# Hybrid encoder step on one core: x loaded first, three cached-key buffers, and another form of the delta rule's norms and sum

## The chip, the cores and the metric

The kernel is one program on one core of one Trainium2 chip. The time is that of one execution on the device, in microseconds; three runs of the kernel before gave 2281.72, 2284.39 and 2290.14 us. The engines are TensorE (PE, with PEld for its weight loads), VectorE (DVE), ScalarE (ACT), GpSimd (POOL) and SyncE (SP, which here only issues DMAs).

## What is computed

One inference step of a one-layer hybrid encoder on 2048 prompt tokens and 8 x 16 sample tokens: an input projection, a gated delta rule (group A, 4 heads), sparse attention whose keys an indexer picks (group B), attention into a memory (group C), and an output projection. The change is in group A and around the sample's indexer. The delta rule, per head and chunk:

```python
kb = k * beta[..., None]
lmat = jnp.where(strict, einsum('bnhid,bnhjd->bnhij', kb, k) * decay, 0.0)
rhs = concatenate([v * beta[..., None], kb * exp(gc)[..., None]], axis=-1)
sol = triangular_solve(lmat + eye(chunk), rhs, left_side=True, lower=True)
u0, wk = sol[..., :dv], sol[..., dv:]
def step(s, xs):
    u = u0_c - einsum('bhcd,bhde->bhce', w_c, s)
    o = einsum('bhcd,bhde->bhce', qd_c, s) + einsum('bhij,bhje->bhie', qk_c, u)
    s = s * last_c[..., None, None] + einsum('bhcd,bhce->bhde', kd_c, u)
```

q and k are first scaled to unit length over their 128 channels. The indexer scores every token t against every key s with `sum_h w[t,h] relu(q_idx[t,h].k_idx[s])`; for the 8 samples s runs over 4096 cached keys each.

## The kernel before

All is float32; a product that must be exact to float32 is made of a high and a low part of each operand (xh, xl, wh, wl, three products). The 17 token tiles of 128 rows (tile 0 holds the samples) go in five groups of 4, 4, 3, 3 and 3 tiles. For each group, 15 steps of projections run (`steps`); each projects into PSUM tile pp and hands on to post-processing. A head's four projections are k, q and then v, z (`t_step`), with channels on the partitions.

The delta rule of a head goes through three stages. **a** (`delta_a`, L991): the squares of k and q are made by ACT from SBUF (sq), a product with a column of ones sums them over the partitions into one column of PSUM tile pa for each tile and operand (pn), DVE takes the reciprocal root; then the decays, Lp (k.k with decay) and at (k.q with decay), and the inverse of each 16 x 16 diagonal block, through DMAs to DRAM and back. **b** (`delta_b`, L1095), for one or two tiles at a time: k is transposed (pk in PSUM tile pb); kw is it times nbe (minus beta, the norm and the decay), kd is it times the decay to the chunk's end; cv is v transposed and scaled; three levels grow the inverse's transpose Z to 128 x 128; nw is the product of kw and Z. **c** (`delta_c`, L1159): for each prompt tile, u = Z.cv + nw.S in PSUM tile pl, then the output and the new state S (Sst). Stage a of head n+2, and its first projections, are recorded only behind stage c of head n.

The samples' index (`idx_sample`, L723) takes 64 blocks of cached keys. `cache_keys` (L701) loads a block (raw, two buffers), ACT copies its high part into kc (two buffers), DVE subtracts the low part, PE multiplies, ACT makes the relu.

The order of the work is fixed when the program is built. Streams (generators) of the stages run against a clock made of a table of costs (`weave`, L173, and `Paced`): the stream that is earliest by it records its next instructions, a yield of some nanoseconds sets it back, and an entry's "lag" (LAG, 600 ns, unless it has its own) is the time that is left between a step and its user. Every engine then takes its instructions in the order of the record, SP its DMAs too. `norms` (L314) sums the squares of x by ACT, half a tile at a time, for the mean over channels; `prep` (L328) scales the transposed x by the result and splits it into xh and xl. L169 is the line of the helper through which all compute instructions are recorded, so rows are told apart by tile names.

After the groups (at some 1550 us) the attention and the output projection follow in pools of their own.

## Time and profile before

| | |
|---|---|
| median of 3 runs | 2284.39 us |
| profiled execution | 2285.57 us |
| its span, first to last instruction | 2283.8 us |
| PE busy | 2006.2 us (88%) |
| DVE busy | 1651.3 us (72%) |
| ACT busy | 1290.8 us (57%) |
| POOL busy | 421.6 us (18%) |
| mean granted TensorE clock | 0.938 of 2.4 GHz |

A busy share is a mean over stretches that differ; the rows below are therefore by stretch, by tile or by time. "Idle before" is the time that the engine stood in front of an instruction, with the one that ended it behind the arrow. Matmuls overlap in the array, so that the mean length of one is more than the time it takes from its engine; a run of several tells the latter.

### The profile page before, as it was taken

How to read it: one execution, taken by the hardware profiler on the slowest of the kernel's cores; microseconds unless marked ns; L12 is line 12 of the kernel's file. 1: busy time of each engine (PE TensorE's matmuls, PEld its weight loads, DVE VectorE, ACT ScalarE, POOL GpSimd, SP SyncE). 2: the span in 40 equal slices, each digit the busy share in tenths (PEclk: the TensorE clock that was granted, in tenths of full speed). 3: DMA queues.
4: the chain of work that ended last, by engine and by line, in shares of the span. 5: the costliest groups of instructions: out<-in, count | busy, mean ns of one | idle time of the engine just before them, and what ended most of it. 6: DMA issues, size and time to landing. Idle time of an engine off the chain costs nothing.

```text
span 2283.8 us, 43471 instructions
## 1 busy us (share of the span) xinstructions
PE 2006.2 (88%) x14123; PEld 1637.8 (72%) x14123; DVE 1651.3 (72%) x6571; ACT 1290.8 (57%) x3193; POOL 421.6 (18%) x494
## 2 busy tenths in 40 slices
PE   3876968688899998999899899989999999999984
PEld 2755746677688888888788888966776666777752
DVE  3766655556888788889988899687767787655541
ACT  3454555445545666566756765456756667545430
POOL 3341512211121101211111111132211121111000
PEclk9886979788999998999899999999999999999996
DMA  7687667866544455556555555547876776765642
GB/s 230 185 246 212 225 156 215 206 224 200 190 162 164 159 183 200 199 192 222 186 212 196 202 193 215 189 138 242 244 227 209 230 222 208 246 207 187 198 137 81
DMA packets 323533, 453.25 MB, mean 198 GB/s; under 512 B 81760, under 2 KB 230880, under 8 KB 303840
## 3 DMA queue, kind: packets, MB, share of 16 engines
q1 hardware_dynamic: 322976, 449.32, 62.2%
q8 instruction: 114, 1.87, 0.3%
q0 software_dynamic: 320, 1.06, 0.2%
q14 instruction: 123, 1.01, 0.1%
HBM read 344.53 MB, written 105.75 MB: 197 GB/s over the span
## 4 chain that ended last, share of the span: by engine, by line


## 5 line engine op out<-in xcount | busy, mean ns | idle before, releaser
L169 PE MATMUL pp<-wh,xh 128*128 128x256 f32 (+1 forms) x952 | 289.3, 304 | 8.5 <-ACT v L169 3.8
L169 PE MATMUL pp<-wl,xh 128*128 128x256 f32 (+1 forms) x952 | 280.3, 295 | 1.2 <-POOL wl L169 1.2
L169 PE MATMUL pp<-wh,xl 128*128 128x256 f32 (+1 forms) x952 | 279.8, 295 | 1.3 <-DVE xl L169 1.3
L169 PE MATMUL pp<-xh,wh 128*128 128x384 f32 (+1 forms) x640 | 249.6, 390 | 10.1 <-ACT wh L169 3.6
L169 ACT ACTIVATE relu<-pi 128x512 f32<-128x512 f32 (+3 forms) x340 | 183.4, 545 | 112.6 <-PE pi L169 65.7
L169 PE MATMUL pp<-xh,wl 128*128 128x384 f32 (+1 forms) x640 | 242.8, 380 | 2.4 <-DMA wl<-wd2l 1.7
L169 DVE SCALAR_TENSOR_TENSOR score<-relu,w,score 128x512 f32<-128x512 f32 (+3 forms) x304 | 221.9, 731 | 30.7 <-ACT relu L169 16.6
L169 PE MATMUL pp<-xl,wh 128*128 128x384 f32 (+1 forms) x640 | 242.8, 379 | 0.0
L169 PEld LDWEIGHTS pp<-wh,xh 128*128 128x128 f32 x952 | 186.2, 196 | 12.9 <-ACT v L169 4.3
L169 PEld LDWEIGHTS pp<-wl,xh 128*128 128x128 f32 x952 | 186.3, 196 | 4.6 <-issue 1.7
L169 PEld LDWEIGHTS pp<-wh,xl 128*128 128x128 f32 x952 | 185.3, 195 | 5.0 <-DVE xl L169 2.5
L169 ACT ACTIVATE junk<-score,tf 128x1024 bf16<-128x1024 f32 (+11 forms) x126 | 142.6, 1132 | 69.0 <-DVE tf L169 45.5
L169 POOL TENSOR_TENSOR Lm<-Lp,cf 128x256 f32<-128x256 f32 (+1 forms) x120 | 85.4, 712 | 309.9 <-PE pb L169 284.1
L169 PE MATMUL pi<-kstack,qst 128*128 128x512 f32 (+3 forms) x304 | 128.4, 430 | 13.9 <-ACT relu L169 11.3
L169 PEld LDWEIGHTS pp<-xh,wh 128*128 128x128 f32 x640 | 125.9, 197 | 20.0 <-ACT wh L169 3.8
L169 PEld LDWEIGHTS pp<-xh,wl 128*128 128x128 f32 x640 | 125.4, 196 | 14.9 <-DMA wl<-wd2l 2.2
L169 PEld LDWEIGHTS pp<-xl,wh 128*128 128x128 f32 x640 | 125.8, 197 | 8.2
L169 PE MATMUL py<-woh,mixh 128*128 128x512 f32 x272 | 122.8, 451 | 3.7 <-ACT mixh L169 3.7
L169 POOL TENSOR_TENSOR wl<-wr,wh 128x512 fp32r<-128x512 f32 (+1 forms) x61 | 81.0, 1336 | 212.3 <-ACT wh L169 205.0
L169 PE MATMUL py<-woh,mixl 128*128 128x512 f32 x272 | 110.7, 407 | 1.8 <-POOL mixl L169 1.8
L169 PE MATMUL py<-wol,mixh 128*128 128x512 f32 x272 | 110.3, 405 | 0.0
L169 POOL TENSOR_TENSOR mixl<-mixr,mixh 128x512 fp32r<-128x512 f32 x33 | 42.3, 1281 | 328.1 <-ACT mixh L169 252.3
(421 smaller groups left out, 5440.1 us busy)
## 6 DMA issues: line engine op xcount, KB each, us to landing
skt<-in_kT SPq DMA_DIRECT2D x128, 256.0 KB
svt<-in_v SPq DMA_DIRECT2D x128, 256.0 KB
nraw<-in_x SPq DMA_DIRECT2D x34, 256.0 KB
xres<-in_x SPq DMA_DIRECT2D x34, 256.0 KB
part_d<-xres SPq DMA_DIRECT2D x34, 256.0 KB
xres<-part_d SPq DMA_DIRECT2D x34, 256.0 KB
out_y<-xres SPq DMA_DIRECT2D x34, 256.0 KB
mixr<-mixT_d SPq DMA_DIRECT2D x33, 256.0 KB
```

The lines of the kernel that those rows point to most:

```text
L169: return f(*args, **kw)
```

## The change

x is loaded first, into eight buffers (tiles of stage a that are free so early), and only the first 512 columns of the constant table follow; the rest and the small tables move into a stream of their own, `small_constants`, and the post-processing is recorded only behind it. The cached keys get a third raw and a third converted buffer, two of the converted ones in columns of kstack, and a lag of 2000 ns. In stage a, k and q are transposed by PE, and ACT's Square sums along each row of the transpose; kd is made there from the same transposes. For prompts kw and nw are gone: stage c forms r = nbe*(k.S) + cv by DVE and u = Z.r. The sample tile keeps kw and nw.

```diff
...
 NX = 2
 EARLY = 14
 NSEL = 256
-PRI1 = (0, 0, 0, 0, 0, 0, 0, 0, 0, 300, 0)
+PRI1 = (0, 0, 0, 0, 0, 0, 0, 0, 0, 0, 300, 0)
 PRI2 = (0, 0, 0, 0, 0, 0, 0, 0, 0)
 MASKED = -(2.0 ** 98)
 BIAS = -(2.0 ** 100)
...
     cpool = ctx.enter_context(tc.tile_pool(name="const", bufs=1))
     dpool = ctx.enter_context(tc.tile_pool(name="scratch", bufs=1, space=DRAM))
     cf = cpool.tile([128, CF_N], F32, name="cf")
-    nc.sync.dma_start(cf, a["cf"])
 
     def C(n):
         return cf[:, CF_COLS[n][0]:CF_COLS[n][1]]
     ident = C("ident")
-    nc.sync.dma_start(g_in, a["g_in"])
...
-    nc.sync.dma_start(cw, a["conv_w"])
-    V.tensor_scalar(cw, cw, 0.5, None, op0=OP.mult)
     g_o = cpool.tile([128, 1], F32, name="g_o")
-    nc.sync.dma_start(g_o, a["g_o"])
-    V.tensor_scalar(g_o, g_o, 0.5, None, op0=OP.mult)
     ab = cpool.tile([128, 8], F32, name="ab")
-    nc.sync.dma_start(ab, a["ab"].to_broadcast([128, 8]))
-    S.activation(ab[:, 0:4], ab[:, 0:4], AF.Exp)
-    V.tensor_scalar(ab[:, 0:4], ab[:, 0:4], -1.0, None, op0=OP.mult)
-    with tc.tile_pool(name="zero", bufs=1) as zp:
-        zero = zp.tile([128, 129], F32, name="zero")
-        G.memset(zero, 0.0)
-        for i in (1, 2):
-            for j in range(2):
-                nc.gpsimd.dma_start(blk_d[i][j].rearrange("t (p r) -> p t r", p=128), zero[:, None, :].to_broadcast([128, 4, 129]))
-
     b1 = ctx.enter_context(ExitStack())
     pi = ctx.enter_context(tc.tile_pool(name="pi", bufs=2, space=PSUM, side="right"))
     tp = ctx.enter_context(tc.tile_pool(name="tp", bufs=1, side="right"))
...
     Sst = gpool.tile([128, 4, 128], F32, name="Sst")
     V.memset(Sst, 0.0)
     gains = gpool.tile([128, 224], F32, name="gains")
-    nc.sync.dma_start(gains, a["gains"].to_broadcast([128, 224]))
-    for o in (0, 128):
-        V.tensor_scalar(gains[:, o:o + 64], gains[:, o:o + 64], 0.125, None, op0=OP.mult)
+
+    def small_constants():
+        yield 4000.0
+        nc.sync.dma_start(cf[:, 512:], a["cf"][:, 512:])
+        nc.sync.dma_start(ab, a["ab"].to_broadcast([128, 8]))
+        nc.sync.dma_start(gains, a["gains"].to_broadcast([128, 224]))
+        nc.sync.dma_start(cw, a["conv_w"])
+        nc.sync.dma_start(g_o, a["g_o"])
+        yield 9000.0
+        S.activation(ab[:, 0:4], ab[:, 0:4], AF.Exp)
+        V.tensor_scalar(ab[:, 0:4], ab[:, 0:4], -1.0, None, op0=OP.mult)
+        for o in (0, 128):
+            V.tensor_scalar(gains[:, o:o + 64], gains[:, o:o + 64], 0.125, None, op0=OP.mult)
+        V.tensor_scalar(cw, cw, 0.5, None, op0=OP.mult)
+        V.tensor_scalar(g_o, g_o, 0.5, None, op0=OP.mult)
+        done["cn"] = 1
     pp = b1.enter_context(tc.tile_pool(name="pp", bufs=2, space=PSUM, side="right"))
     pa = b1.enter_context(tc.tile_pool(name="pa", bufs=1, space=PSUM))
     pb = b1.enter_context(tc.tile_pool(name="pb", bufs=1, space=PSUM))
...
         ss = xp.tile([128, 5, 2], F32, name="ss")
         for t in range(n):
             for e in range(2):
-                xt = np_.tile([128, 512], F32, name="nraw")
+                if gi:
+                    xt = np_.tile([128, 512], F32, name="nraw")
+                else:
+                    xt = dp.tile([128, 4, 128], F32, name="xrow", tag=("Lp", "at", "X", "Z")[t]).rearrange("p a b -> p (a b)")
                 nc.sync.dma_start(xt, a["x"][(g0 + t) * 128:(g0 + t + 1) * 128, e * 512:e * 512 + 512])
                 S.activation(xt, xt, AF.Square, accum_out=ss[:, t, e:e + 1])
+        if gi == 0:
+            nc.sync.dma_start(cf[:, :512], a["cf"][:, :512])
+            nc.sync.dma_start(g_in, a["g_in"])
         sm = xp.tile([128, 5], F32, name="ssm")
         V.tensor_tensor(sm[:, :n], ss[:, :n, 0], ss[:, :n, 1], op=OP.add)
         V.tensor_scalar(sm[:, :n], sm[:, :n], 1.0 / D, EPS, op0=OP.mult, op1=OP.add)
...
         tp = keys["tp"]
 
         def fetch(i):
-            raw = keys["sc"][:, 1536:2048] if i % 2 else tp.tile([128, 512], F32, name="kraw", tag="junk")
+            raw = keys["sc"][:, 1536:2048] if i % 3 == 1 else tp.tile([128, 512], F32, name="kraw", tag=("junk", "", "far")[i % 3])
             nc.sync.dma_start(raw, a["kidxT"][order[i % 8], :, i // 8 * 512:i // 8 * 512 + 512])
             return raw
-        raws = [fetch(0), fetch(1)]
+        raws = [fetch(i) for i in range(3)]
         yield 3500.0
         for i in range(64):
-            yield from until(lambda: keys["n"] >= i - 1)
-            kc = tp.tile([128, 512], F32R, name="kc", tag=("qn", "far")[i % 2])
+            yield from until(lambda: keys["n"] >= i - 2)
+            kc = kstack[:, 512 + 512 * (i % 3):][:, :512] if i % 3 else tp.tile([128, 512], F32R, name="kc", tag="qn")
             S.activation(kc, raws[i], AF.Copy)
             yield 1
             V.tensor_tensor(kc[64:128], raws[i][64:128], kc[64:128].bitcast(F32), op=OP.subtract)
-            keys["k"].append({"x": kc})
+            keys["k"].append({"x": kc, "lag": 2000.0})
             yield keys["k"][-1]
-            if i + 2 < 64:
-                raws.append(fetch(i + 2))
+            if i + 3 < 64:
+                raws.append(fetch(i + 3))
 
     def idx_sample(tp, pl, top):
         yield from until(lambda: done["i"] > 0)
...
     def head_proj(n_, h, gi, w, parts_, R, hp):
+            yield from until(lambda: done["cn"])
...
         gs = slice(g0, g0 + n)
 
-        pn = pa.tile([128, 512], F32, name="pa")
+        ms = dp.tile([128, 12], F32, name="dms")
+        kd = dp.tile([128, 4, 128], F32, name="kd")
         for i, x in enumerate((k, q)):
-            for lo, hi in units(gi):
-                sq = t3(dp, "sq", hi - lo, bufs=2)
-                S.activation(sq, x[:, lo:hi], AF.Square)
-                yield 1
-                for t in range(lo, hi):
-                    T.matmul(pn[:, i * n + t:i * n + t + 1], sq[:, t - lo, :], C("one")[:, 0:1], start=True, stop=True)
-                yield 0
-        ms = dp.tile([128, 12], F32, name="dms")
-        V.tensor_scalar(ms[:, :2 * n], pn[:, :2 * n], EPS, None, op0=OP.add)
+            pn = p3(pa, n)
+            for t in range(n):
+                T.transpose(pn[:, t, :], x[:, t, :], ident)
+            yield 1
+            for t in range(n):
+                sq = dp.tile([128, 128], F32, name="sq", bufs=2)
+                S.activation(sq, pn[:, t, :], AF.Square, accum_out=ms[:, i * n + t:i * n + t + 1])
+                if i == 0:
+                    S.activation(kd[:, t], pn[:, t, :], AF.Copy, scale=esuf[:, g0 + t, h:h + 1])
+            yield 1
+        V.tensor_scalar(ms[:, :2 * n], ms[:, :2 * n], EPS, None, op0=OP.add)
         rr = dp.tile([128, 12], F32, name="drr")
         rsqrt(rr[:, :2 * n], ms[:, :2 * n], dp, "d%d" % n)
         rk, rq = rr[:, :n], rr[:, n:2 * n]
...
             Lms.append(Lm)
         for lv in levels[:2]:
             level(lv)
-        kw, kd, cv = t3(dp, "kw", m, bufs=1), t3(dp, "kd", m), t3(dp, "cv", m)
-        pk = p3(pb, m)
-        for t in range(m):
-            T.transpose(pk[:, t, :], k[:, lo + t, :], ident)
-        yield 1
-        V.tensor_tensor(kw, pk, nbe[:, lo:hi, None].to_broadcast(shp), op=OP.mult)
-        for t in range(m):
-            S.activation(kd[:, t], pk[:, t, :], AF.Copy, scale=esuf[:, g0 + lo + t, h:h + 1])
-        yield 1
+        cv = t3(dp, "cv", m)
+        if smp:
+            kw = dp.tile([128, 128], F32, name="kw", bufs=1)
+            pk = p3(pb, 1)
+            T.transpose(pk[:, 0, :], k[:, 0, :], ident)
+            yield 1
+            V.tensor_scalar(kw, pk[:, 0, :], nbe[:, 0:1], None, op0=OP.mult)
+            yield 1
         pv = p3(pb, m)
         for t in range(m):
             T.transpose(pv[:, t, :], v[:, lo + t, :], ident)
...
             if li == 0:
                 level(levels[2])
             yield 1
-        pw = p3(pb, m)
-        for t in range(m):
-            T.matmul(pw[:, t, :], kw[:, t, :], Zg[:, t, :], start=True, stop=True)
-        yield 1
-        nw = t3(dp, "nw", m)
-        S.activation(nw, pw, AF.Copy)
-        R[lo] = Zg, kd, cv, nw
+        nw = None
+        if smp:
+            pw = p3(pb, 1)
+            T.matmul(pw[:, 0, :], kw, Zg[:, 0, :], start=True, stop=True)
+            yield 1
+            nw = dp.tile([128, 1, 128], F32, name="nw", bufs=1)
+            S.activation(nw, pw, AF.Copy)
+        R[lo] = Zg, R["kd"][:, lo:hi], cv, nw
         yield 1
 
     def delta_c(gi, h, lo, hi, R, dp):
 
         g0, n = GROUPS[gi]
-        q, z = (R[x][:, :n * 128].rearrange("p (t c) -> p t c", c=128) for x in "qz")
-        at, rq = R["at"], R["rq"]
+        k, q, z = (R[x][:, :n * 128].rearrange("p (t c) -> p t c", c=128) for x in "kqz")
+        at, rq, nbe = R["at"], R["rq"], R["nbe"]
         Zg, kd, cv, nw = R[lo]
         m = hi - lo
         smp = g0 + lo == 0
...
             St = Sst[:, h, :]
             for t in range(m):
                 pu = pl.tile([128, 512], F32, name="pl")[:, :128]
-                T.matmul(pu, Zg[:, t, :], cv[:, t, :], start=True, stop=False)
-                T.matmul(pu, nw[:, t, :], St, start=False, stop=True)
+                T.matmul(pu, k[:, lo + t, :], St, start=True, stop=True)
                 T.matmul(pout[:, t, :], q[:, lo + t, :], St, start=True, stop=False)
+                yield 1
+                r = dp.tile([128, 128], F32, name="r")
+                V.scalar_tensor_tensor(r, pu, nbe[:, lo + t:lo + t + 1], cv[:, t, :], op0=OP.mult, op1=OP.add)
+                yield 1
+                pu = pl.tile([128, 512], F32, name="pl")[:, :128]
+                T.matmul(pu, Zg[:, t, :], r, start=True, stop=True)
                 yield 1
                 u = dp.tile([128, 128], F32, name="u")
                 S.activation(u, pu, AF.Copy)
...
     def post(items, key):
+        yield from until(lambda: done["cn"])
...
         done["end"] = 1
 
     norms(0, xp)
+    zero = dp.tile([128, 129], F32, name="zero", tag="Lb", bufs=1)
+    G.memset(zero, 0.0)
+    for i in (1, 2):
+        for j in range(2):
+            nc.gpsimd.dma_start(blk_d[i][j].rearrange("t (p r) -> p t r", p=128), zero[:, None, :].to_broadcast([128, 4, 129]))
 
     def index():
         yield from memory_keys(tp, pi)
         yield from idx_sample(tp, pi, SLOT)
         yield from idx_prompt(range(3, EARLY), tp, pi, SLOT)
-    weave(tc, log, *zip((stage_c(), stage_b(), post(posts_t, "tp"), post(posts_n, "n"), stage_a(), splits(), loads(),
+    weave(tc, log, *zip((small_constants(), stage_c(), stage_b(), post(posts_t, "tp"), post(posts_n, "n"), stage_a(), splits(), loads(),
           index(), cache_keys(), prep(xp), projections()), PRI1))
     nc.sync.dma_start(a["pconv"], hist)
     nc.sync.dma_start(a["pssm"].rearrange("h d e -> d h e"), Sst)
```

SP's list at the start, before: the tables (cf, g_in, cw, g_o, ab, gains), x in pairs (nraw), weight pieces (wr), the memory's inputs.

```order
L217 DMA cf<-in_cf 128x1874
L223 DMA g_in<-in_g_in 128x8
L257 DMA cw<-in_conv_w 128x48
L260 DMA g_o<-in_g_o 128x1
L263 DMA ab<-in_ab 128x8
L286 DMA gains<-in_gains 128x224
L320 DMA nraw<-in_x 128x512 x2
L371 DMA wr<-in_w_n 128x512 x3
L320 DMA nraw<-in_x 128x512 x2
L802 DMA g_mem<-in_g_mem 128x8
L804 DMA g_km<-in_g_km 128x256
```

And after:

```order
L320 DMA xrow<-in_x 128x512 x8
L323 DMA cf<-in_cf 128x512
L324 DMA g_in<-in_g_in 128x8
L374 DMA wr<-in_w_n 128x512 x3
L805 DMA g_mem<-in_g_mem 128x8
L807 DMA g_km<-in_g_km 128x256
L346 DMA xr<-in_xT 128x2x256
L814 DMA mraw<-in_w_mem 128x512
L816 DMA mT<-in_memT 128x256
L346 DMA xr<-in_xT 128x2x256
L273 DMA cf<-in_cf 128x1362
L274 DMA ab<-in_ab 128x8
```

x stands in front, and cf's second part, ab, gains, cw and g_o between the loads of transposed x (xr).

DVE's list after the reciprocal root of x, before (xr scaled, xl the low part, mT and mhl of the memory's keys):

```order
L169 TENSOR_SCALAR xr<-cf,rstd 128x128 x4
L169 TENSOR_SCALAR mT<-mT,g_mem 128x256
L169 TENSOR_TENSOR mhl<-mT,mhl 128x256
L169 SCALAR_TENSOR_TENSOR xr<-xr,g_in,rb 128x256 x3
L169 TENSOR_TENSOR xl<-xr,xh 128x2x256
L169 SCALAR_TENSOR_TENSOR xr<-xr,g_in,rb 128x256
L169 TENSOR_SCALAR mT<-mT,g_mem 128x256
L169 TENSOR_TENSOR xl<-xr,xh 128x2x256
L169 TENSOR_TENSOR mhl<-mT,mhl 128x256
```

And after:

```order
L169 TENSOR_TENSOR xl<-xr,xh 128x2x256
L169 SCALAR_TENSOR_TENSOR xr<-xr,g_in,rb 128x256 x2
L169 TENSOR_TENSOR mhl<-mT,mhl 128x256
L169 TENSOR_TENSOR xl<-xr,xh 128x2x256
L169 TENSOR_SCALAR ab<-ab 128x4
L169 SCALAR_TENSOR_TENSOR xr<-xr,g_in,rb 128x256 x2
L169 TENSOR_SCALAR gains<-gains 128x64 x2
L169 TENSOR_SCALAR cw<-cw 128x48
L169 TENSOR_TENSOR xl<-xr,xh 128x2x256
L169 SCALAR_TENSOR_TENSOR xr<-xr,g_in,rb 128x256 x2
L169 TENSOR_SCALAR g_o<-g_o 128x1
```

The steps on ab, gains, cw and g_o now stand between the scalings of xr.

PE's list in the middle of a group, two tiles of stage c among the other streams (pb is stage b, pp the projections, pa stage a, pi the index), before:

```order
L169 MATMUL pa<-q,k 128x128
L169 MATMUL pi<-kstack,qst 128x384
L169 MATMUL pb<-Z,Lm 128x128
L169 MATMUL pi<-kstack,qst 128x384
L169 MATMUL pl<-cv,Z 128x128
L169 MATMUL pl<-Sst,nw 128x128
L169 MATMUL po<-Sst,q 128x128
L169 MATMUL pb<-Y,X 128x128
L169 MATMUL pi<-kstack,qst 128x384
L169 MATMUL pl<-u,kd 128x128
L169 MATMUL po<-u,at 128x128
```

And after:

```order
L169 MATMUL pp<-xh,wh 128x384
L169 MATMUL pl<-Sst,k 128x128
L169 MATMUL po<-Sst,q 128x128
L169 MATMUL pb<-Z,Lm 128x128
L169 MATMUL pb<-cf,Z 128x128
L169 MATMUL pl<-r,Z 128x128
L169 MATMUL pp<-xl,wh 128x384
L169 MATMUL pp<-xh,wl 128x384
L169 MATMUL pb<-Y,X 128x128
L169 MATMUL pl<-u,kd 128x128
L169 MATMUL po<-u,at 128x128
L169 MATMUL pp<-xh,wh 128x384
```

The product with the state (Sst,k) and the one with the inverse (r,Z) now have three matmuls of other work between them, in which DVE has to make r; before, the two products into pl stood back to back.

## Rows read from the trace of the kernel before

**Rows 1.** Busy us by stretch: stretch, length, each engine (instructions), clock, DMA, GB/s.
```profile
0.00:20.00 20.00, 0.00 (x0) 0.00 (x0) 1.30 (x11) 5.61 (x12) 6.92 (x14) 1.00 0.83 209
...
0.00:600.00 600.00, 459.95 (x2491) 368.21 (x2492) 367.06 (x1200) 300.11 (x703) 156.81 (x173) 0.85 0.73 210
...
600.00:1500.00 900.00, 836.26 (x5594) 758.94 (x5593) 775.12 (x3677) 545.18 (x1379) 133.81 (x203) 0.97 0.55 188
...
100.00:400.00 300.00, 238.52 (x1280) 177.05 (x1279) 188.51 (x537) 155.67 (x356) 87.55 (x91) 0.85 0.75 206
```

**Rows 2.** Instructions by time, first 42 us: start, us, engine, what, [idle before].
```profile
10.39 0.15 DVE L169 TENSOR_SCALAR g_o<-g_o 128x1 f32<-128x1 f32 x1 [3.38 <-DMA g_o<-in_g_o]
...
13.99 0.20 ACT L169 ACTIVATE ab<-ab 128x4 f32<-128x4 f32 x1 [11.95 <-DMA ab<-in_ab]
...
15.13 0.63 ACT L169 ACTIVATE nraw<-nraw 128x512 f32<-128x512 f32 x1 [0.94 <-DMA nraw<-in_x]
...
28.55 0.63 ACT L169 ACTIVATE nraw<-nraw 128x512 f32<-128x512 f32 x1 [1.17 <-DMA nraw<-in_x]
...
30.50 1.21 DVE L169 SCALAR_TENSOR_TENSOR rstd<-x_b,rstd 128x4 f32<-128x4 f32 x1
...
35.48 2.08 PE L169 MATMUL pp<-xr,cf 128*128 128x128 f32 x8 [4.95 <-DVE xr L169]
...
41.50 0.62 PE L169 MATMUL pp<-wh,xh 128*128 128x304 f32 x1
```

**Rows 3.** Who waited for whom, 100 to 420 us: total us, times, longest.
```profile
PE pi L169 <- DVE kc L169: 30.0, 19, 6.4
...
ACT kc L169 <- DMA kraw<-in_kidxT: 7.0, 9, 1.3
...
ACT kc L169 <- DMA score<-in_kidxT: 4.7, 5, 1.6
```

**Rows 4.** Instructions by time, PE, two of the key matmuls.
```profile
132.12 0.50 PE L169 MATMUL pi<-kc,qst 128*128 128x512 f32 x1 [1.68 <-DVE kc L169]
...
303.48 0.79 PE L169 MATMUL pi<-kc,qst 128*128 128x512 f32 x1 [6.36 <-DVE kc L169]
```

**Rows 5.** Groups, 60 to 1560 us: count, busy us, mean ns, idle before, releasers.
```profile
L169 PE MATMUL pa<-cf,sq 128*128 128x1 f32 x272 | 40.5, 248 | 16.9 <-ACT sq L169 16.8
...
L169 PE MATMUL pi<-kc,qst 128*128 128x512 f32 x64 | 33.6, 525 | 30.6 <-DVE kc L169 30.0
...
L169 PE MATMUL pl<-u,kd 128*128 128x128 f32 x128 | 28.9, 309 | 0.5 <-ACT u L169 0.4
...
L169 ACT ACTIVATE o<-po 128x128 f32<-128x128 f32 x88 | 24.2, 276 | 17.5 <-PE po L169 16.7
...
L169 DVE SCALAR_TENSOR_TENSOR Sst<-Sst,last,pl 128x128 f32<-128x128 f32 x64 | 21.8, 341 | 13.9 <-PE pl L169 13.5
...
L169 PE MATMUL pl<-cf,o 128*128 128x128 f32 x68 | 17.1, 310 | 14.9 <-DVE o L169 10.8 <-DVE tf L169 3.3 <-DVE Xs L169 0.4
...
L169 ACT ACTIVATION_READ_ACCUMULATOR o<-po 128x1 f32 x68 | 13.5, 198 | 0.0
...
L169 DVE SCALAR_TENSOR_TENSOR score<-relu,w,score 128x512 f32<-128x512 f32 x168 | 133.6, 796 | 16.5 <-DMA score<-in_epsrow 8.7 <-ACT relu L169 6.0 <-DVE score L169 0.5
```

**Rows 6.** Instructions by time, PE, around 1020 us, in stage a.
```profile
1018.06 0.53 PE L169 MATMUL pa<-cf,sq 128*128 128x1 f32 x4
...
1018.77 0.28 PE L169 MATMUL pa<-cf,sq 128*128 128x1 f32 x2
...
1026.39 0.61 PE L169 MATMUL pa<-cf,glog 128*128 128x128 f32 x4
```

**Rows 7.** Busy time by stretch of sq alone, then of kw alone (sum rows).
```profile
600.00:1560.00 960.00, 26.60 (x192) 29.31 (x192) 20.71 (x60) 0.97 0.56 189
...
sum 1560.00, PE 40.47 PEld 44.14 ACT 29.75; mean PE 20.24 PEld 22.07 ACT 14.87
...
sum 1560.00, PE 24.69 PEld 19.27 DVE 15.63; mean PE 12.35 PEld 9.63 DVE 7.82
```

More of the change, by code (lines that the diff above doesn't have):

```diff
@@ L307, in rsqrt @@
         V.scalar_tensor_tensor(y, t, 0.5625, y, op0=OP.add, op1=OP.mult)
-    done = dict.fromkeys(("a", "b", "c", "i", "t", "s", "n", "na", "tp", "ta", "w", "end", "m", "k", "sv", "smp", "nm", "x", "xf", "bl", "sx"), 0)
+    done = dict.fromkeys(("a", "b", "c", "i", "t", "s", "n", "na", "tp", "ta", "w", "end", "m", "k", "sv", "smp", "nm", "x", "xf", "bl", "sx", "cn"), 0)
     done["xf"] = 1
@@ L1091, in delta_a @@
         nc.sync.dma_start(Z[:, :n], full(Zd))
-        R.update(Lp=Lp, at=at, X=X, Z=Z, cc=cc, nbe=nbe, rq=rq)
+        R.update(Lp=Lp, at=at, X=X, Z=Z, cc=cc, nbe=nbe, rq=rq, kd=kd)
         yield 6000.0
```

## Prediction

> **What bounds the kernel now.** I read the busy times by stretch first. From 600 to 1500 us PE is busy 836.3 of 900 us (93%), at a granted clock of 0.97; DVE 775.1 (86%), ACT 545.2 (61%) [rows 1]. The attention behind some 1550 us the change leaves almost as it is. So in the long middle of the recorded phase work taken off PE is worth nearly its size, as long as DVE, right behind it, gets no more. The first 600 us are another regime: PE busy 460 of 600 us at a clock of 0.85, the DMA engines busy 73% of the time [rows 1]. Here three things end PE's waits: the start (nothing to multiply until 35.48 us, the first projection at 41.50) [rows 2], the cached keys of the sample index (30.0 us of PE waiting for DVE's half of a key block, the longest entry there of PE's matmuls) [rows 3], and the delta rule's own hops. Every engine takes its work in the recorded order, so a wait in front of one key block holds all that stands behind it.
>
> **Start: x first, constants later.** Before, the 960 KB constant table and five small tables go ahead of x, and x has two buffers: its first half tile is squared at 15.13 us and the last at 28.55; the reciprocal root, ten small DVE steps with single ones of 1.2 us beside POOL's work, ends in PE's first matmul on it at 35.48 [rows 2]. After, eight x buffers are free at once and SP issues all eight loads (2 MB) first, then 256 KB of the table. At the 209 GB/s of the first 20 us [rows 1], shared with the 1 MB of zeros that POOL's queue writes in both kernels, 3.3 MB take some 16 us. The last Square then ends near 17 instead of 29.2, prep's first matmul stands near 21 and the first projection near 27 instead of 41.50: 14 us less. Three weight pieces, g_mem, g_km and an xT piece are queued behind x and set the 27. What is given back: the rest of the table and four small loads now lie between the xT pieces, and DVE's list has ab, gains, cw and g_o between the scalings of x, ACT's list has ab's Exp between its copies to xh. Before, ab came 3.6 us after g_o, each alone [rows 2]; one such arrival on which DVE or ACT has to wait delays the scalings behind it, and so the projections, by that much. Bounds: all 14 us, or 14 less three such waits (11), 3. I take 10, a little over one wait.
>
> **Cached keys: three buffers.** The third raw buffer, the third converted one (two of the three now in columns of kstack that prompts write only from group 2 on, after 800 us) and a plan lag of 2000 instead of 600 ns put each key matmul later in PE's list than its DVE half. PE waits 30.6 us in all before the 64 key matmuls [rows 5]; eight of these waits are over 1.4 us, 21.5 us together, the first (1.68) and the longest (6.36) stand in [rows 4]. If the lag alone shifts each by 1.4 us, those eight keep 10.3 us and the rest vanish: 20 us less. ACT's waits for the key DMAs themselves are 11.7 us [rows 3], which the third buffer should mostly end. What is late next is the DMA queue (75% busy between 100 and 400 us [rows 1]) and the chain of head n+2, whose first projections are recorded only behind stage c of head n. Bounds 0 and 30; I take 18.
>
> **Norms from transposed tiles.** Gone: 136 one-column products, 272 PE instructions, and their Squares from SBUF on ACT, 29.75 us [rows 7]. New: one transpose for k and one for q for each of 68 tile-heads, 136, of which 64 take over the transposes that stage b loses; net 72. Four one-column instructions last 0.53 us and two 0.28, so each costs 0.125 us; four of 128 columns last 0.61, 0.11 each over one's 0.28 [rows 6]. PE: 272 x 0.125 = 34.0 less, 72 x 0.11 = 7.9 more (I take a transpose as one such instruction). The row shows that one column costs as much as 128, because the weights change each time. The Trainium skill, TensorE: Matmul & The Clock Gate, Back-to-back issue gap, gives matmuls of up to 64 columns some 25 ns; by that the removal would be worth 6.8 us instead of 34.0 and the whole sum about 16 us smaller, near 2250. The trace is of this very instruction, so its 0.125 stands. ACT gets 136 Squares that read PSUM, as o<-po 0.276 us with an accumulator read of 0.198 [rows 5], 64 us for the 29.75 and for nw's copies (13.5): ACT is 61% busy, and the cover is PE's and DVE's work; without it the delta norms of a head come 1 to 2 us later. kd moves from b to a with the same instructions; POOL's kdb, queued behind it, gets it earlier.
>
> **The inverse behind the sum.** Gone for prompts: the product of kw and the inverse (64 products, 128 PE instructions, 128 x 0.115 = 14.7 us), its copy nw, and kw on DVE (15.63 us, of which some 1.1 stay for the sample [rows 7]). The two products that formed u from cv and nw become k.S and inverse.r, so PE keeps their count. New: 64 DVE steps r = pu*nbe + cv, nearest row the state update of the same shape from PSUM, 0.341 us [rows 5]: 21.8 us; DVE net +7.3. The chain of a chunk gets one hop longer (PE, DVE r, PE), and stage b loses two (kw, nw): lengths about cancel. But r is a new place for PE to wait, with the projections of all streams queued behind it; usually the order has three to five matmuls, 0.4 to 0.9 us, in between. Bounds: 0.5 us in all, as at pl<-u,kd behind ACT's copy, or 0.22 for each, as at pl<-cf,o behind DVE's o (14.9 over 68) [rows 5], 14. I take 4, since r's operands are ready earlier than o's.
>
> **Sum.** PE gets 34.0 - 7.9 + 14.7 = 40.8 us less. About 0.7 of it lies after 600 us (192 of the 272 one-column instructions [rows 7]), where PE is 93% busy: 28, of which I count 24; of the 12 before, where PE idles anyway, 4. Minus 4 for r: 24. With 10 and 18: 52 us. Against the profiled execution of 2285.57 us (span 2283.8, 1.8 us around it; 1.2 over the median of 2284.39, inside the runs' spread) that gives **2234 us**.
>
> **Rivals.** (B) DVE is the bound. In 600 to 1500 us it is 86% busy, PEld 84% [rows 1]; if DVE's list sets the pace there, PE's gain is not collected and r's 7.3 us are paid: 2286 - 28 + 7 = **2265**. For it: PE's waits at pl<-cf,o end on DVE [rows 5]. Against: DVE itself is idle 125 us in that stretch, PE only 64. The Trainium skill, Perfetto Trace Analysis, Identifying the Most-Contended Engine, says not to judge TensorE by matmul busy time but by weight loading; by that DVE is the tighter engine and this rival is the forecast. No row here decides it. (C) The first 600 us are set by the DMA queue and the chain of heads, so that an earlier x and earlier keys only wait elsewhere: 2286 - 24 = **2262**. For it: DMA at 75%; against: PE waits for keys that have landed. That the third buffer does not help, because the plan spaces the keys closer, belongs here. (D) r stalls the chain: slower. If each of the 64 steps finds a score step of 0.80 us [rows 5] in progress on DVE and PE stands for both, 64 x 1.14 = 73 us are lost: 2286 - 56 + 73 = **2303**. It turns slower from 0.87 us for each r; 0.22 is the worst such row. (E) More: earlier keys bring stage c of heads 0 and 1 forward, projections of heads 2 and 3 follow, and the first 600 us lose half of their 140 us of PE idle instead of 28: 70 + 20 = 90, **2196**.
>
> **Chances.** Forecast 0.52, B 0.17, C 0.13, D 0.07, E 0.11. The range takes in E, B and C and leaves D out: 2195 to 2268. A measurement of this kernel tells about 0.5% from no change, here 11 us: B lies near that bound. Faster by more 0.84, within 0.10, slower 0.06.
>
> **What would show it.** Right: PE's first matmul near 21 us and the first projection before 30; idle before key matmuls under 13 us; no pa<-cf,sq, in its place pa<-cf,k and pa<-cf,q with 136 instructions; PE busy 35 to 45 us less in all with its share after 600 us still over 90%; idle before pl<-r,Z under 10 us in all. Wrong: PE's share after 600 us down to 88% with DVE's over 90% (B); key waits gone but the projections of heads 2 and 3 no earlier than now (C); pl<-r,Z among the longest waits (D); DVE or ACT standing more than 8 us before cw, gains or ab (the start).

## The result, and the profile after

The changed kernel takes 2245.51 us (median; 2234.17 to 2253.76) beside 2283.05 before: ratio 0.9835, interval 0.9806 to 0.9863, that is 38 us less (31 to 44). The forecast was 52 less, 2234, with 2195 to 2268 around it. The time lies in the range and the direction is right, but of the three terms the start was half of what was forecast and the delta rule more than half as much again. A second series (r_after, below) gave 0.9799 (0.9773 to 0.9824), 46 us less. How wide one kernel scatters is seen from its two profiled executions, mean granted clock beside the span, of the first series and of the second:

```profile
core 0: 2252.0 us, clock 0.938
```
```profile
core 0: 2237.1 us, clock 0.944
```

PE's busy time over the whole span (columns as in [rows 1]), first series, then second:

```profile
0.00:2290.00 2290.00, 1971.46 (x13795) 1607.35 (x13795) 1661.57 (x6595) 1284.28 (x3337) 418.45 (x494) 0.94 0.62 198
```
```profile
0.00:2290.00 2290.00, 1957.40 (x13795) 1593.87 (x13795) 1661.84 (x6595) 1282.41 (x3337) 417.25 (x494) 0.94 0.62 198
```

The same 13795 instructions take 14.1 us longer at the lower clock. Span less busy, PE's idle time, is 280.5 and 279.7. Of the 14.9 us between the two, 14.1 lie in PE's busy time. DVE shows 1661.6 and 1661.8. In this one pair, then, idle time agrees to a microsecond and PE's busy time differs by 14; a difference in busy time between profiles of two kernels is to be read with that in mind.

By stretch, changed kernel (answers to [rows 1]):

```profile
0.00:600.00 600.00, 459.40 (x2513) 372.72 (x2514) 392.92 (x1294) 314.31 (x800) 162.40 (x177) 0.87 0.73 217
600.00:1500.00 900.00, 831.69 (x5481) 743.27 (x5479) 794.54 (x3714) 551.14 (x1505) 143.35 (x215) 0.97 0.56 192
```

PE's share after 600 us is still 92%, DVE's rose from 86% to 88%. In the whole span PE is busy 34.7 us less (2006.2 before), idle 280.5 instead of 277.6: PE's relief is in the time, and in sum no idle time is gone. That sum hides two parts: with the delta rule alone PE idles 292.1 us (e_delta below), and the keys take some 12 to 16 of that away again. For the start, see PE's instructions of the changed kernel by time (as [rows 2]):

```profile
21.52 2.08 PE L169 MATMUL pp<-xr,cf 128*128 128x128 f32 x8 [21.52 <-DVE xr L169]
26.92 2.93 PE L169 MATMUL pi<-mw,mhl 128*128 128x512 f32 x6 [3.33 <-ACT mhl L169]
...
35.15 0.80 PE L169 MATMUL pi<-mw,mhl 128*128 128x512 f32 x1 [5.30 <-ACT mhl L169]
36.45 2.50 PE L169 MATMUL pi<-mw,mhl 128*128 128x512 f32 x5 [0.51 <-POOL mw L169]
38.75 0.46 PE L169 MATMUL pp<-wh,xh 128*128 128x304 f32 x1
```

and DVE's:

```profile
34.29 0.35 DVE L169 TENSOR_SCALAR mT<-mT,g_mem 128x256 f32<-128x256 f32 x1 [1.33 <-DMA mT<-in_memT]
```

The first matmul on x came 14 us earlier, as forecast (21.52 for 35.48). The first projection came 2.75 us earlier (38.75 for 41.50), not 14: ahead of it in PE's list stand the products of the memory's keys (pi<-mw,mhl), and their next input, the next piece of mT, lands in front of 34.29. Before the change PE did these first, while it had nothing on x:

```profile
25.65 4.88 PE L169 MATMUL pi<-mw,mhl 128*128 128x512 f32 x12 [25.65 <-ACT mhl L169]
```

That piece of mT is late because of its place in SP's list. Its issue, before and after:

```profile
21.72 0.43 SPq L813 DMA_DIRECT2D mT<-in_memT  x1
```
```profile
30.63 0.44 SPq L816 DMA_DIRECT2D mT<-in_memT  x1
```

Now three loads of transposed x, which wait for buffers (the first of them 6.7 us, for PE's first matmul on x), and the small tables stand ahead of it.

Who waited for whom, 100 to 420 us (answers to [rows 3]):

```profile
PE pi L169 <- DVE kstack L169: 17.7, 8, 8.8
...
ACT kc L169 <- DMA kraw<-in_kidxT: 9.7, 4, 4.3
ACT kstack L169 <- DMA score<-in_kidxT: 9.2, 5, 5.0
ACT kstack L169 <- DMA kraw<-in_kidxT: 5.0, 3, 2.9
```

PE's waits for a key block's DVE half went from 30.0 to 17.7 us, and ACT's for the loads grew from 11.7 to 23.9. The growth need not be the third buffer's: with the delta rule and two buffers (e_delta) ACT waits 29.4 us for them. Groups of 60 to 1560 us (answers to [rows 5]):

```profile
L169 ACT ACTIVATE sq<-pa 128x128 f32<-128x128 f32 x136 | 38.2, 287 | 13.2 <-PE pa L169 13.0
L169 PE MATMUL pl<-r,Z 128*128 128x128 f32 x128 | 27.3, 296 | 4.6 <-DVE r L169 4.4
L169 DVE SCALAR_TENSOR_TENSOR r<-pl,dnbe,cv 128x128 f32<-128x128 f32 x64 | 21.9, 343 | 4.6 <-PE pl L169 3.7
L169 PE MATMUL pl<-cf,o 128*128 128x128 f32 x68 | 16.7, 306 | 16.8 <-DVE o L169 14.7 <-DVE xt L169 1.3 <-DVE tmp L169 0.5
L169 PE MATMUL pa<-cf,k 128*128 128x128 f32 x68 | 13.4, 301 | 8.3 <-DVE k L169 3.9 <-ACT last L169 2.8 <-ACT lasts L169 1.6
L169 PE MATMUL pa<-cf,q 128*128 128x128 f32 x68 | 12.1, 296 | 5.8 <-DVE q L169 3.2 <-ACT kd L169 2.5
```

The 16.9 us that PE stood before pa<-cf,sq [rows 5] are gone. Before the transposes that took their place it stands 14.1, half of it for k and q themselves and the rest for ACT. r costs what was forecast, in length (343 ns) and in waits (4.6 us).

### The profile page after: what moved, and what is told of

Read it like the earlier page. It is cut to its first block, busy times and chain, and to the rows that moved or that the text cites. A ratio compares the mean times of both kernels' runs of the same rounds, so it can differ in the third digit from the quotient of the medians.

```text
span 2252.0 us, 42965 instructions
## 1 busy us (share of the span) xinstructions
PE 1971.5 (88%) x13795; PEld 1607.3 (71%) x13795; DVE 1661.6 (74%) x6595; ACT 1284.3 (57%) x3337; POOL 418.5 (19%) x494
## 4 chain that ended last, share of the span: by engine, by line
PE 37%; DVE 20%; DMA 6%; ACT 4%; issue 3%; SPq 1%; POOL 0%; DVEq 0%; ACTq 0%; POOLq 0%
PE py L169 10%; PE pp L169 6%; PE pt L169 5%; PE pi L169 4%; PE po L169 4%; DVE score L169 4%; PE ps L169 3%; PE pb L169 2%; DVE tmp L169 1%; PE pl L169 1%; ACT junk L169 1%; SPq L1674 1%; PE pa L169 1%; DMA svt<-in_v 1%; DVE k L169 1%
## 5 line engine op out<-in xcount | busy, mean ns | idle before, releaser
L169 PE MATMUL pi<-kstack,qst 128*128 128x512 f32 (+3 forms) x346 | 151.6, 448 | 35.7 <-DVE kstack L169 17.7
L169 PEld LDWEIGHTS pi<-kstack,qst 128*128 128x128 f32 x346 | 68.0, 198 | 67.8 <-ACT relu L169 30.1
```

What stands on the lines that cost most here:

```text
L169: return f(*args, **kw)
```

## The experiments

Two theories. **Mine**: three independent terms, start 10, keys 18, delta rule 24, the last by PE's work after 600 us. **Rivals**: DVE sets the pace (B); start and keys feed one later limit (C). Microseconds are worked out from the ratio and the median of the kernel before that was run beside it; where two such differences are compared, the range comes from both intervals, taken as independent.

**e_start.** The hunks on the constants, small_constants, x's buffers and the loads alone:

```diff
-                xt = np_.tile([128, 512], F32, name="nraw")
+                    xt = dp.tile([128, 4, 128], F32, name="xrow", tag=("Lp", "at", "X", "Z")[t]).rearrange("p a b -> p (a b)")
...
+        nc.sync.dma_start(cf[:, 512:], a["cf"][:, 512:])
```

> The kernel before with the start alone changed (x first into eight buffers, constants behind it); keys and delta rule as before. By my forecast the 14 us of an earlier first matmul stay, less one late constant: 10 us faster (3 to 14). The changed kernel's trace supports it: its first matmul on x stands at 21.54 us instead of 35.48, its last projection comes 49 us earlier. Rival (the first 600 us are set by the DMA queue and the chain of heads): the reciprocal root of group 0 comes 14 us earlier, but the first head's output (272.2 us in the kernel before) stays within 4 us, and the whole within 4 us.

Measured: 2279.58 beside 2283.91, 0.9978 (0.9962 to 0.9993), 5 us faster (2 to 9). The first head's last output stands at 305.4 us for 307.6. Between the two theories, nearer to the rival.

**e_keys.** The hunks in cache_keys alone:

```diff
-            kc = tp.tile([128, 512], F32R, name="kc", tag=("qn", "far")[i % 2])
+            kc = kstack[:, 512 + 512 * (i % 3):][:, :512] if i % 3 else tp.tile([128, 512], F32R, name="kc", tag="qn")
...
-            keys["k"].append({"x": kc})
+            keys["k"].append({"x": kc, "lag": 2000.0})
```

> The kernel before with the third raw and converted key buffers and the lag of 2000 ns alone. By my forecast the waits in front of the 64 key matmuls fall from 30.6 us to about 10 and the whole is 18 us faster (0 to 30). Rival: the waits fall as much, but what stands behind them waits elsewhere, so that PE's idle time of the first 600 us (140 us) falls by less than 8 us and the whole changes by less than 6.

Measured: 2266.26, 0.9911 (0.9883 to 0.9939), 20 us faster (14 to 27). The size was right; the waits in front of the key matmuls fell from 30.6 only to 20.4. PE's idle time of the whole span fell by about as much, from 277.6 to 266.7.

**e_start_keys.** Both.

> Start and keys together, delta rule as before. If the two take away different waits, the sum of the two runs alone, by my forecast 28 us faster. If both feed the same later limit (the DMA queue, the chain of heads), no more than the larger of the two, 14 to 18 us. The two traces so far are in favour of the first: head 3's first output is 47 us earlier in the changed kernel, and 26 us are left at 600 us.

Measured: 2266.66, 0.992 (0.9897 to 0.9943), 18 us faster (13 to 24). No more than the keys alone by the medians. The sum of the two alone, 25, is not excluded by intervals of this width, so this run does not decide between one limit and two.

**e_delta.** The hunks in delta_a, delta_b and delta_c alone:

```diff
+                T.transpose(pn[:, t, :], x[:, t, :], ident)
...
+                    S.activation(kd[:, t], pn[:, t, :], AF.Copy, scale=esuf[:, g0 + t, h:h + 1])
...
+                V.scalar_tensor_tensor(r, pu, nbe[:, lo + t:lo + t + 1], cv[:, t, :], op0=OP.mult, op1=OP.add)
```

> The norms from transposed tiles and the inverse behind the sum alone, start and keys as before. By my forecast PE's busy time falls by 40.8 us (traces: pa, pb and pl together fell by 40.5) and the time by 24. If DVE sets the pace of 600 to 1500 us (rival B), PE idles more by as much as it is relieved and the time falls by less than 6. The two traces so far: from the reciprocal root of group 1 on the changed kernel wins only some 7 us more, so I lean to 10 us faster.

Measured: 2245.79, 0.983 (0.9805 to 0.9854), 39 us faster (33 to 45): as much as the whole change. My reading of the two traces (most of the gain before 600 us, so start and keys) was wrong: this kernel has no part of either and reaches the reciprocal root of group 2 (groups counted from 0; its copy rb on ACT is the mark in the trace) just as early, at 594.6 us for 623.0. Of the 40 us between the two profiles 28 lie ahead of that root and 12 behind it.

**e_norm.** Norms from the transposes, but k transposed again in stage b, for kd and kw:

```diff
+                T.transpose(pn[:, t, :], x[:, t, :], ident)
...
         kw, kd, cv = t3(dp, "kw", m, bufs=1), t3(dp, "kd", m), t3(dp, "cv", m)
```

> The kernel before with the norms alone from transposed tiles (k transposed once more in stage b, kd and kw as before). PE saves 34.0 - 15.6 (136 transposes more) = about 18 us. By my forecast's way of counting 0.7 of that counts: 12 us faster. If instead stage a's shorter way to the reciprocal root (first square to it 7.8 us in the run of the delta rule alone, 14.5 before, in head 0) shortens the chain of heads, group 1's root (623.0 us before, 594.6 there) comes 10 us or more earlier already here, and most of the 38 us of the delta rule would stand by this part: 20 or more.

Measured: 2286.35 beside 2285.09, 0.9995 (0.9976 to 1.0014): nothing. Group 2's root (the expectation calls it group 1's) comes 28 us earlier (595.4) and the end does not: behind that root this kernel takes 1687.0 us, the kernel before 1660.8. Of these 26 us, 21 are PE standing idle (152.3 us there for 131.2). An early root alone is therefore no gain.

**e_rec.** The inverse behind the sum; kd from stage b, norms as before:

```diff
-        kw, kd, cv = t3(dp, "kw", m, bufs=1), t3(dp, "kd", m), t3(dp, "cv", m)
+        kd, cv = t3(dp, "kd", m), t3(dp, "cv", m)
```

> The kernel before with the inverse behind the sum alone (kw and nw gone for prompts, r made by DVE, norms as before). PE saves 14.7 us, DVE pays 7: by my forecast's way 10 - 4 = 6 us faster, by a bound DVE (rival B) 0 to 7 slower. If stage b's two hops less (kw, and the product with its copy nw) shorten the chain of heads in the first 600 us, group 2's root comes 10 us or more earlier and the time falls by 15 or more.

Measured: 2272.98, 0.995 (0.9929 to 0.9972), 11 us faster (6 to 16). Not slower; group 2's root hardly moves (619.1). This alone does not speak against B, for DVE's busy time in this profile is 1642.1 us, 9 less than before, r's steps and all. e_delta does: there DVE works 13 us more (1664.5 for 1651.3) and the kernel is 39 us faster; behind group 2's root alone DVE has 12 us more work and the kernel takes 12 us less.

**e_delta_kdb.** Both of these, kd still in stage b:

```diff
+        kd, cv = t3(dp, "kd", m), t3(dp, "cv", m)
+        pk = p3(pb, m)
+        for t in range(m):
+            T.transpose(pk[:, t, :], k[:, lo + t, :], ident)
```

> Norms from transposed tiles and the inverse behind the sum together, but k's second transpose and kd stay in stage b; start and keys as before. Alone the two parts gave 0 and 11 us, together with kd moved to stage a 38. If the missing 27 us come from the move of kd (a step less in stage b, 64 transposes less on PE), this run is 11 to 15 us faster than before, about 2271. If they come from the two parts meeting (each alone leaves the other's wait in place), it is near the delta rule's full 38, about 2248 or 7 us of transposes above: 2253.

Measured: 2274.12 beside 2288.26, 0.9934 (0.9909 to 0.9959), 15 us faster (9 to 21). The missing 24 of the 39 (16 to 32 by the two intervals) come with the move of kd to stage a. Without the move group 2's root stands at 617.2 us, with it at 594.6.

**e_delta_pe.** The delta rule's change with 64 transposes and 64 products put back on PE, into columns that nobody reads:

```diff
+        if not smp:
+            for t in range(m):
+                T.transpose(pv[:, 2 + t, :], k[:, lo + t, :], ident)
...
+            if li == 2:
+                for t in range(m):
+                    T.matmul(pz[:, 2 + t, :], k[:, lo + t, :], k[:, lo + t, :], start=True, stop=True)
```

> The delta rule's change alone (norms, sum, kd in stage a), with PE work put back for which no engine waits: in stage b k is transposed once more for the 64 prompt chunks and 64 products of k with itself are written where nothing reads them. That is 22 us of PE's work, as many instructions as the moved kd and the removed product of kw and the inverse gave up. If PE's work is what counts, as in my forecast, the time is 15 to 22 us longer than with the delta rule alone: some 2262 to 2268. If the shorter steps of stages a and b count and not PE's work, it stays within 6 us: 2240 to 2252.

Measured: 2258.65, 0.9874 (0.9848 to 0.99), 29 us faster (23 to 35): 10 less than without the extra work (2 to 18 by the two intervals), between the two theories. Busy time over the whole span, without and with it:

```profile
0.00:2290.00 2290.00, 1951.45 (x13795) 1591.87 (x13795) 1664.52 (x6595) 1287.93 (x3337) 418.97 (x494) 0.94 0.62 198
```
```profile
0.00:2290.00 2290.00, 1975.73 (x13987) 1609.52 (x13987) 1662.52 (x6595) 1285.84 (x3337) 422.80 (x494) 0.94 0.62 198
```

192 instructions and 24.3 us more on PE, at nearly the same clock (0.942 and 0.941), but spans of 2243.5 and 2250.8: PE's idle time fell from 292.1 to 275.1. By the medians PE's work is worth some 0.4 of its size (10 of 24.3); the intervals leave 0.1 to 0.75, so not nearly all.

**e_delta_start** and **e_delta_keys.** The delta rule with the start, and with the keys, hunks as above.

> The changed kernel with the keys as before: start and delta rule. The delta rule alone gave 38 us and the whole change 38. If the start has its own 4 us (as alone), 42 us faster, 2242; if the start is lost as soon as the delta rule is faster, 38.

> The changed kernel with the start as before: keys and delta rule. If keys and delta rule shorten the same waits (the chain of heads of the first 600 us), no more than the delta rule alone: 38 us faster. If they are independent, 38 + 18 = 56, and it is the start that spoils the whole change by 18 us.

Measured: 2236.12, 0.9778 (0.9755 to 0.9801), 51 us faster; and 2244.95, 0.9811 (0.9788 to 0.9834), 43 us. Beside the delta rule's 39, the start adds 12 (4 to 20) and the keys 4 (-3 to 12), where alone they gave 5 and 20. What is plain is that the keys' 20 are not there a second time.

**e_after_lag** and **r_after.** The changed kernel without the lag of its own, and the changed kernel again:

```diff
-            keys["k"].append({"x": kc, "lag": 2000.0})
+            keys["k"].append({"x": kc})
```

> The changed kernel with the key matmuls' lag at its default of 600 ns instead of 2000, three buffers kept. If the lag is what the three buffers cost beside an early start (keys later than they need be), the time falls to that of the changed kernel without the key part, 2236. If the buffers alone take the waits away, it is no different from the changed kernel, 2245; the waits in front of the key matmuls (19.7 us in the changed kernel, kept in kstack and qn) come back to over 25 if the lag was what shifted them.

> The changed kernel again, in the same call as the others. Without the key part it took 2236.1 us (ratio 0.9778, interval 0.9755 to 0.9801), with it 2245.5 (0.9835, 0.9806 to 0.9863), in runs of different calls. If the key part costs time in company, this run gives a ratio over 0.980 again; if the difference was the call's, under 0.980.

Measured: 2248.36, 0.9823 (0.9796 to 0.985), and 2242.61, 0.9799 (0.9773 to 0.9824). The waits in front of the key matmuls are 28.6 us without the lag and 19.9 with it; the times cannot be told apart. Nor is the kernel without the key part (2236.12) told apart from this second series: the intervals overlap from 0.9773 to 0.9801. From the first series (0.9806 to 0.9863) it is. So the key part is shown to bring nothing measurable in company; whether it costs stays open.

## Why the keys and the delta rule do not add

The sum that does not come out is that of the keys and the delta rule: 20 and 39 us alone, 43 together. The traces show two things that bear on it; that either is the cause is not shown.

**The first is SP's list.** SP issues its DMAs in the recorded order, the key loads among them, and each of those waits until its buffer is read. Behind them stands the store of Lp, with which a head's inverse begins. SP's longest wait of 100 to 420 us, before:

```profile
SPq L708 <- DVE kc L169: 64.8, 29, 6.8
```

and the answering ones of the changed kernel:

```profile
SPq L711 <- DVE kc L169: 25.0, 8, 9.9
SPq L711 <- DVE kstack L169: 21.3, 12, 5.2
```

What SP's list does to head 0, before (DVE makes the last Lp, SP issues its store):

```profile
147.51 0.35 DVE L169 SCALAR_TENSOR_TENSOR Lp<-pa,dbp,e 128x128 f32<-128x128 f32 x1 [0.71 <-PE pa L169]
```
```profile
186.10 0.42 SPq L1067 DMA_DIRECT2D blk<-Lp  x1
```

The store's own row is 0.42 us long and shows no wait, and yet it is 38 us late. Key loads are only a part of what SP waited for meanwhile (148 to 186.2 us, the three longest):

```profile
SPq L320 <- ACT nraw L169: 8.8, 4, 5.0
SPq L940 <- DMA out_sconv<-raws: 4.6, 1, 4.6
SPq L708 <- DVE kc L169: 4.5, 3, 2.5
```

In e_start the same two rows:

```profile
139.49 0.35 DVE L169 SCALAR_TENSOR_TENSOR Lp<-pa,dbp,e 128x128 f32<-128x128 f32 x1
```
```profile
182.73 0.42 SPq L1071 DMA_DIRECT2D blk<-Lp  x1
```

Lp is ready 8 us earlier, its store goes out 3.4 us earlier: here much of the rest of the start's gain stays behind. (That a row shows less than the wait is also what the Trainium skill says, Perfetto Trace Analysis, Per-instruction lifecycle: semaphore waits and the transfer itself lie outside the window that a DMA instruction's row brackets. The trace agrees: 0.42 us for 38.)

When the store of Lp goes out for the four heads of group 0, key loads ahead of the stores of heads 0 and 1 in SP's list, ACT's copy rb of group 2, and PE's busy and idle time of the whole span, all from the traces, in us:

| kernel | stores, heads 0 to 3 | key loads ahead | group 2's rb | PE busy | PE idle |
|---|---|---|---|---|---|
| before | 186, 291, 396, 505 | 16, 38 | 623.0 | 2006.2 | 277.6 |
| e_start | 183, 288, 390, 501 | 16, 38 | 616.2 | 2002.3 | 273.9 |
| e_keys | 183, 288, 384, 475 | 17, 41 | 606.5 | 2002.7 | 266.7 |
| e_start_keys | 185, 291, 384, 475 | 17, 41 | 603.6 | 2000.1 | 269.7 |
| e_norm | 156, 267, 376, 462 | 12, 31 | 595.4 | 1990.9 | 291.5 |
| e_rec | 184, 293, 404, 491 | 16, 38 | 619.1 | 1985.9 | 280.1 |
| e_delta_kdb | 162, 277, 392, 480 | 12, 32 | 617.2 | 1976.4 | 300.3 |
| e_delta | 161, 268, 378, 471 | 12, 31 | 594.6 | 1951.5 | 292.1 |
| e_delta_start | 161, 266, 378, 470 | 12, 31 | 591.9 | 1944.4 | 293.1 |
| e_delta_keys | 160, 258, 368, 464 | 14, 34 | 597.9 | 1968.2 | 275.6 |
| changed kernel | 160, 258, 368, 463 | 14, 34 | 596.5 | 1971.5 | 280.5 |
| r_after | 159, 256, 367, 459 | 14, 34 | 589.8 | 1957.4 | 279.7 |

The stores do overlap: head 3's goes out 30 us earlier with the keys, 34 with the delta rule and 41 with both. In the kernels with the new norms the store is recorded earlier, and fewer key loads stand ahead of it. By what way the keys bring head 3's forward is not seen. SP waits for their buffers as long in e_keys as before (36.2 us on kstack and 27.3 on kc, for 64.8; the changed kernel's 46.3 are the delta rule's, 45.8 in e_delta), and the stores of heads 0 and 1 gain only 3 us. Nor is an early store enough: e_delta_kdb has head 3's 25 us earlier and group 2's root only 6, and e_norm has an early root and no gain at the end. No run moved the store in SP's list alone.

**The second is where PE's time goes.** The keys lower PE's idle time in company too: by 11 us alone, by 16 beside the delta rule, by 13 beside the delta rule and the start, each time about as much as the waits in front of the key matmuls fall (10, 12 and 14). Beside the start alone it is 4, where those waits fall by 12. What rises in company is PE's busy time for the same 13795 instructions. Over the whole span, e_delta_keys, to be read beside e_delta's row above:

```profile
0.00:2290.00 2290.00, 1968.20 (x13795) 1605.00 (x13795) 1662.52 (x6595) 1282.69 (x3337) 416.88 (x494) 0.94 0.62 198
```

and e_delta_start, to be read beside the two of the changed kernel:

```profile
0.00:2290.00 2290.00, 1944.37 (x13795) 1584.93 (x13795) 1665.45 (x6595) 1287.17 (x3337) 419.11 (x494) 0.95 0.62 198
```

PE is busy 17 us longer with the keys than without them (1951.5), and with the start 13 and 27, at a lower granted clock (0.937 for 0.942; 0.944 and 0.938 for 0.949). Alone the keys do not lengthen it (2006.2 and 2002.7). So in these profiles the waits went and did not come back as waits; busy time took their place. With one profile of most kernels, and 14 us between two of the same, why that is so stays open. One rival is untested throughout: every edit also changes the order in which all streams are recorded (in e_keys ten of PE's 14123 instructions change sides of group 2's root).

## Why the prediction was right or wrong, point by point

- **What bounds the kernel: half right.** The two regimes are there. But that PE's work after 600 us is worth nearly its size is not borne out: 24.3 us put back cost 10 (2 to 18; 7 between the two profiles). Neither does DVE set the pace: e_delta gives it 13 us more and is 39 us faster. Both stand between 86 and 93% busy, and what one engine gives up is in part taken up in waits for the others: with the delta rule alone PE is busy 54.7 us less and idle 14.4 us more. Rival B, which would have collected nothing of PE's relief, was as far off on the other side. The Trainium skill, Perfetto Trace Analysis, Identifying the Most-Contended Engine, judges TensorE by its weight loads and VectorE by its busy share; by that DVE is the tighter one in the changed kernel (88%, for PEld's 83%, 743.3 of 900 us). The runs do not agree that it sets the time.
- **Start: the failed step is "the first projection near 27".** First matmul right (21.52), first projection 38.75. I had followed x alone, and not what stands between prep and the projections in PE's list. That PE had "nothing to multiply until 35.48 us" was a misreading: it multiplied the memory's keys from 25.65 us on, and with x first these come later. Then SP's list takes most of the rest. The give-back that I priced, DVE or ACT waiting for late small constants, did not come: DVE does not stand at all before ab, gains or cw. It stands 1.33 us before mT, whose load those tables and the loads of x now precede. 5 us alone for 10, inside the bounds of 3 and 14.
- **Keys: the sum right by two wrong steps.** Alone 20 us for 18. But the waits fell by 10, not 20 ("the rest vanish"), and ACT's waits for the loads, "which the third buffer should mostly end", rose from 11.7 to 20.6 in e_keys (beside the delta rule they fell, from 29.4 to 23.7). PE's idle time fell by 11 us; where the rest of the 20 comes from is not shown. Beside the delta rule the gain is gone, and rival C has the outcome right for this part, key waits down and the whole no faster, though not the way: PE's idle time did fall, and its busy time rose.
- **Delta rule: mechanism right on PE, the largest term missing.** PE's busy time of pa, pb and pl together went from 451.3 to 410.7 us (127.6, 213.7, 110.0 to 116.7, 178.5, 115.6): 40.6 less for 40.8, and 50.0 less in e_delta's profile. The trace's 0.125 us for a one-column instruction carried that. (With the 25 ns of the Trainium skill, TensorE: Matmul & The Clock Gate, Back-to-back issue gap, it would have been 13.6, an estimate. The section gives that figure for isolated matmuls and says that its formula "under-counts" at few columns, where each matmul has a weight load of its own; the trace, at 0.125 us, agrees with the warning, not with 25 ns.) Its worth was probably oversized, 24 where 0.4 of 40.6 would be 16, an estimate from e_delta_pe. The term left at nothing was the move of kd, which the prediction had as "the same instructions": 39 us came, 24 of them with it. The place was wrong too: 24 us were forecast after 600 us and 4 before, and 28 came ahead of group 2's root and 12 behind it. The move takes 64 transposes off PE (some 7 us by the prediction's 0.11 each) and one round trip (transposes in the one buffer of pb, ACT's copies, next transposes) out of stage b, on the way to the next head. What of the 24 is work and what is the round trip, the runs don't separate.
- **r: right.** 4.6 us of waits before pl<-r,Z for 4; rival D (2303) has nothing for it.
- **Rival E: right in kind, in part.** The first 600 us contracted, by 26.5 us at group 2's root, though not by earlier keys as it had it: the delta rule alone does as much (28.4).
- **The total.** 10 + 18 + 24 = 52 was forecast; alone the parts give 5 + 20 + 39 = 64, together 38 to 46. A delta rule sized too small and an overlap left out nearly cancel. That is luck, and by it alone the time lies as near to the forecast as it does.
- **What would show it.** Right: the first matmul, 136 instructions in pa<-cf,k and pa<-cf,q, PE's share of 92%, PE busy 34.7 us less (48.8 in the second profile, for 35 to 45), r. Wrong: the first projection, the key waits (20.5 for 13).
- **Open.** Why the norms alone lose behind group 2's root, mostly in idle time of PE, what they win ahead of it. Why the keys' gain is gone beside the delta rule. Why the start gives 12 us beside the delta rule and 5 alone: PE's idle time is no lower there (293.1 for 292.1), but its granted clock is higher, 0.943 to 0.949 in the five executions of e_delta_start and 0.937 to 0.942 in the five of e_delta, so that part of the 12 may be the clock's.

## What to carry to other kernels

A queue that issues DMAs in a fixed order is an engine like the others: look for the time between a tile's last write and the issue of its store, since the store's own row does not show it, and count what stands ahead of it. Parts priced alone need not add, so price each with the others already done. A step moved out of a chain with one buffer can be worth more than the work it carries: here 24 us for some 7 us of PE's. And an earlier mark in the middle of a kernel, like group 2's root, is no gain until the end is seen to move.

## What the runs showed of the hardware

TensorE's granted clock changes between 1.2 and 2.4 GHz within one execution, and differently in each. Two profiles of the same program, 0.938 and 0.944 in the mean, differ by 14.9 us, 14.1 of it in PE's busy time, with idle time equal to a microsecond. The mean clock is not all of the scatter: one execution of e_start took 2277.96 us at 0.939, another 2282.71 at 0.941.

The start of the clock differs too. 33 to 43 us, before, then the changed kernel in its first and its second series:

```profile
33.00:43.00 10.00, 6.50 (x19) 4.75 (x19) 7.68 (x13) 2.72 (x6) 4.92 (x4) 0.51 0.50 148
```
```profile
33.00:43.00 10.00, 6.52 (x18) 4.96 (x18) 7.76 (x9) 4.39 (x8) 5.68 (x4) 1.00 0.74 236
```
```profile
33.00:43.00 10.00, 6.01 (x18) 4.55 (x18) 7.83 (x10) 4.53 (x9) 5.52 (x4) 0.66 0.77 237
```

PE is about as busy in all three. The first stretch is almost wholly at 1.2 GHz and the second at 2.4, which looks like a gain of the early start; but the third is the same program as the second and has 0.66. One profile does not tell what a change does to the clock of so short a stretch. Over the first 600 us the three were granted 0.85, 0.87 and 0.88. In the mean of whole executions e_start had 0.942 (twelve) and the kernel beside it 0.939 (seventeen); that the early start is the cause is not shown.
